# Reordering the seven block products of a second feed-forward product, and building their partner operands in one temporary

## The chip, the cores and the metric

The kernel runs on one core of a Trainium2 chip. The metric is the device time of one execution in microseconds (us); lower is better. TensorE (PE) multiplies, VectorE (DVE), ScalarE (ACT) and GpSimd (POOL) work elementwise, and SyncE (SP) issues most of the transfers.

## The reference

Two encoder layers over 1024 tokens of width 1024, in float32. Layer 0 mixes tokens by windowed attention, layer 1 by a gated linear recurrence (HGRN2); each mixer also has four cross-attention heads into 256 memory tokens. Every layer ends in a feed-forward part with a depthwise convolution of width 3 over tokens. Cut to what matters here:

```python
def conv_ffn(v, w_in, conv_w, conv_b, w_out):          # w_in 1024 x 5632, w_out 2816 x 1024
    gate, up = jnp.split(v @ w_in, 2, axis=-1)
    hid = jax.nn.gelu(dwconv_centred(gate, conv_w, conv_b)) * up
    return hid @ w_out

for layer in range(2):
    u = rmsnorm(h, norm_g[layer, 0])
    y = mixer(u)                                       # layer 0 window attention, layer 1 HGRN2
    h = h + rmsnorm(y, norm_g[layer, 1])
    f = conv_ffn(rmsnorm(h, norm_g[layer, 2]), ...)
    h = h + rmsnorm(f, norm_g[layer, 3])
```

## The kernel before

Every operand of a matmul is split into a rounded high part and the remainder (`wh`/`wl`, `uh`/`ul`: one cast on ACT and one subtraction on DVE), and a float32 product is made of three matmuls, high-high, high-low and low-high.

The program runs start(), window() (layer 0's mixer), its output projection, ffn(0), hgrn() (layer 1's mixer), its output projection and ffn(1). The code gives the instructions in program order; a planner that replays a timeline sets the final order on each engine and lets later work move ahead where its buffers are free. Tiles live in pools that are stacked from the left or the right of SBUF and PSUM, and a pool that is laid on the place of a released one waits tile by tile until the old tiles have been read.

**First feed-forward product** (first_units). The 1024 x 1024 normalised tokens stand transposed in `uh`, `ul`. The first two of 22 column blocks (f = 0, 1) are plain products (plain()). From f = 2 on each block of 128 gate and 128 up columns is computed as seven block products of 12 matmuls (a form of Strassen's method): prod(k, ...) for k = 1, 2, 5, 6, 7, 3, 4. They accumulate in PSUM banks X, V and Y, which ACT or DVE reads between some of them. Their token operands `B[k]` are blocks of `uh`/`ul` or sums of them, made by operands() during f = 0; `B[5]` is written back over a block of `uh`/`ul` at f = 1, once the plain products have read it. Their weight operands are sums too: load(f) brings raw blocks into tiles `sx` and `sy` (two buffers each) by SyncE, and three accumulating DMAs on POOL's queue add to them, one after another; weights() then splits `a1`, `sx`, `sy` and `a22` into ring buffers. conv() and hidden() make the hidden block and store it, with the sums that the second product needs, in DRAM (`hd`).

operands() uses, for each of two halves, three temporaries that take the tags of other tiles: `t3` takes `sy`, `t2` takes `c`, `t4` takes `sx`.

**Second feed-forward product.** The 1024 x 2816 by 2816 x 1024 product is again seven block products M1 to M7, in the order `SECOND`, each over NP2 = 11 units of 256 contraction rows: unit() loads one weight block (or a weight sum made earlier) and one hidden block and splits both; mms() then does 3 matmuls for each of four token tiles t. Four PSUM banks `Xs` stand on the right and four `Vs` on the left. With signs folded into the operands, the quadrants of the result are

```text
c11 = M1 + M2              (early sums:  M1)
c12 = M1 + M6 + M5 + M3    (             M1 + M6)
c22 = M1 + M6 + M7 + M5    (             M1 + M6 + M7)
c21 = M1 + M6 + M7 + M4
```

where c11 and c21 make up the token half `ia`, c12 and c22 the half `ib`. In the order 1 5 6 3 7 2 4, products 1, 6, 7 and 4 accumulate in `Xs`, 5 and 3, and then 2, in `Vs`; between two products on one set of banks lies a product on the other. The half `ib` is complete after product 7, and its four tail() calls (load of the residual rows, scale by the reciprocal root mean square, add, store) run during product 2. The half `ia` ends with product 4: its last LAST units are held back and applied token tile by token tile, so that each tile's tail starts as soon as its own bank is complete. HOLD of the held units have a pool of their own; the others stand in the ring.

In layer 0 (gnext) tail() also normalises the rows for layer 1, and transposes them through a PSUM pool `pst` into `uh`, `ul` (norm_T). `pst` is opened on the left once `Vs` is released after product 2; the transposes of half `ib` are put off to the first units of product 4 (halt, turns). hgrn() then opens its projection banks `psj` (two) on the left and six other banks on the right. Its first work is proj(0): v01 (values and gates of rows 0 to 511), q0, f0 for the first half, then v23, q1 and the rest.

Of the kernel before, what the change touches and what calls it, by code (L numbers as in the profile page):

```python
# [16 lines left out]
P = 128  # L17
# [21 lines left out]
ORD = ["V v01 QF q0 f0 v23 B q1 b1 f1 b0"] + ["QFB q0 f0 q1 b1 f1 b0 v0123"] * 6 + ["QFVB q0 f0 v01 v23 q1 b1|f1|b0"]  # L39


LAST = (7, 10)
HOLD = (5, 8)

PLAIN = 2

# [1 line left out]
def build(tc, A, out):  # L48
# [37 lines left out]
    def split(h, l, src):  # L86
        act.copy(h, src)  # L87
        dve.tensor_tensor(l, src, h.bitcast(F32), op=ALU.subtract)  # L88
# [16 lines left out]
        nc.sync.dma_start(g, src_row.to_broadcast([P, D]))  # L105
        return g

    def norm_T(pl, pst, src, g, dh, dl, t, tag="n", ub=2, halt=False):
        ss = pl.tile([P, 1], F32, tag=tag + "ss", name=tag + "ss")
        u = pl.tile([P, D], F32, tag=tag + "u", bufs=ub, name=tag + "u")  # L110
        sumsq(pl, src, ss, u)
        rs = rstd_of(pl, ss, 1, D, tag)
        dve.scalar_tensor_tensor(u, src, rs[:, 0:1], g, op0=ALU.mult, op1=ALU.mult)
        def turn(pst):
            for b in range(2):
                ps = pst.tile([P, 4, P], F32, tag="pt", name="pt")
                for k in range(4):
                    pe.transpose(ps[:, k, :], u[:, (4 * b + k) * P:(4 * b + k + 1) * P], ident)  # L118
                split(dh[:, 4 * b:4 * b + 4, t * P:(t + 1) * P],
                      dl[:, 4 * b:4 * b + 4, t * P:(t + 1) * P], ps)  # L120

        if halt:
            return turn
        turn(pst)

    w2sum = [dram.tile([NP2, 4, P, 512], F32, name=f"w2s{l}") for l in range(2)]

# [406 lines left out]
    def ffn(l, wo, dst, gnext, halves_, out_halves):  # L534
# [51 lines left out]
        def operands():  # L586

            b12 = (uh[:, :4, tj], ul[:, :4, tj])
            late = []
            for kk in range(2):  # L590
                ks = slice(2 * kk, 2 * kk + 2)
                f32 = lambda x: x[:, ks].bitcast(F32)
                def tmp(t, b=1):
                    return fp.tile([P, 2, 512], F32, tag=t, bufs=b, name=t)
                def both(o, x, y, sub):
                    q = tmp("tt", 2)
                    dve.tensor_tensor(o, f32(x[0]), f32(y[0]), op=ALU.subtract)
                    dve.tensor_tensor(q, f32(x[1]), f32(y[1]), op=ALU.subtract)
                    dve.tensor_tensor(o, o, q, op=ALU.add)
                def more(o, a_, x, op):  # L600
                    dve.tensor_tensor(o, a_, f32(x[0]), op=op)
                    dve.tensor_tensor(o, o, f32(x[1]), op=op)
                t3, t2, t4 = tmp("sy", 2), tmp("c", 3), tmp("sx", 2)
                both(t3, B[3], b12, True)
                split(B[7][0][:, ks], B[7][1][:, ks], t3)
                more(t2, t3, B[1], ALU.add)
                nsplit(B[6][0][:, ks], B[6][1][:, ks], t2)
                more(t4, t2, B[2], ALU.subtract)
                split(B[4][0][:, ks], B[4][1][:, ks], t4)
                e1 = tmp("u") if kk else tmp("g")  # L610
                both(e1, B[1], b12, True)
                late.append((ks, e1))
            return late
# [122 lines left out]
                yield  # L736


        SECOND = (1, 5, 6, 3, 7, 2, 4)
        where = {1: (2, None), 2: (3, None), 4: (1, None), 5: (None, 0), 7: (None, 1), 6: (None, 2), 3: (None, 3)}  # L740
        todo = [(k, p) for k in SECOND for p in range(NP2)]
        made = []
# [1 line left out]
        def unit(k, p):  # L744
            r = stg.tile([P, 2, 512], F32, tag="st", name="st")
            a_, d_ = where[k]
            nc.sync.dma_start(r[:, 0, :], A["ffw2"][l, p, a_] if d_ is None else w2d[p][d_])
            nc.sync.dma_start(r[:, 1, :], hd[k, p])
            pl = hold_pool if k == 4 and 0 <= p - (NP2 - LAST[l]) < HOLD[l] else ring
            h, l_ = [pl.tile([P, 1024], F32R, tag=t, name=t) for t in ("wh", "wl")]  # L750
            r = r.rearrange("p a b -> p (a b)")
            if k == 6:
                nsplit(h[:, :512], l_[:, :512], r[:, :512])
                split(h[:, 512:], l_[:, 512:], r[:, 512:])
            else:
                split(h, l_, r)
            return h, l_

        def second_ahead():
            if todo and len(made) < (LAST[l] if todo[0][0] == 4 else 3):  # L760
                made.append(unit(*todo.pop(0)))

        for _ in first_units():
# [13 lines left out]
        g3 = grow(np_, A["norm_g"][l, 3:4, :], "g3")  # L777
        g0 = grow(np_, A["norm_g"][l + 1, 0:1, :], "g0") if gnext else None
        dve.tensor_scalar_mul(g3[:, 512:], g3[:, 512:], -1.0)
        y = {q: yp.tile([P, 4, 512], F32, name=q) for q in ("c11", "c12", "c22")}  # L780
        ss = {q: yp.tile([P, 4], F32, name=q) for q in ("q11", "q12", "q22")}
        Xs = {t: psl.tile([P, 512], F32, tag=f"x{t}", name="X") for t in (2, 3, 0, 1)}
        Vs = None
        tok = lambda b, t: slice((4 * b + t) * P, (4 * b + t + 1) * P)

        def tail(b, t, ya, sa, yb, sb):


            ts_ = tok(b, t)
            x = np_.tile([P, D], F32, tag="x", bufs=2, name="x")  # L790
            nc.sync.dma_start(x, h1d[l][ts_, :])
            sq = np_.tile([P, 1], F32, tag="sq", name="sq")
            dve.tensor_tensor(sq, sa, sb, op=ALU.add)
            rs = rstd_of(np_, sq, 1, D, "p")
            last = not gnext and b == out_halves[0] and t == 3
            for c, yy in ((slice(0, 512), ya), (slice(512, 1024), yb)):
                dve.scalar_tensor_tensor(x[:, c], yy, rs[:, 0:1], x[:, c], op0=ALU.mult, op1=ALU.add)
                if last:
                    (nc.sync if c.start == 0 else act).dma_start(dst[ts_, c], x[:, c])
            if not last:  # L800
                nc.sync.dma_start(dst[ts_, :], x)
            if gnext:
                return norm_T(np_, pst, x, g0, uh, ul, 4 * b + t, ub=4, halt=True)

        def scaled(q, n, c):

# [8 lines left out]

        ia, ib = out_halves
        D0, D1 = slice(0, 512), slice(512, 1024)
        pst, turns = None, []
        for k in SECOND:
            if k in (5, 2):  # L820
                Vs = [psr.tile([P, 512], F32, tag="v", name="V") for _ in range(4)]
            ps = Xs if k in (1, 6, 7, 4) else Vs
            hold = []
            for p in range(NP2):
                while len(made) < 1:
                    second_ahead()
                h, l_ = made.pop(0)
                second_ahead()
                if k == 4 and p >= NP2 - LAST[l]:
                    hold.append((p, h, l_))  # L830
                else:
                    mms(k, p, h, l_, ps, range(4), k in (1, 5, 2) and p == 0)
                if k == 2 and p in (2, 4, 6, 8):
                    t = p // 2 - 1
                    turns.append(tail(ib, t, y["c12"][:, t, :], ss["q12"][:, t:t + 1],
                                      y["c22"][:, t, :], ss["q22"][:, t:t + 1]))
                if k == 4 and gnext and p < 4:
                    turns.pop(0)(pst)
            for t in range(4):
                if k == 1:  # L840
                    act.copy(y["c11"][:, t, :], Xs[t])
                elif k == 5:
                    act.copy(y["c22"][:, t, :], Vs[t])
                elif k == 6:
                    act.copy(y["c12"][:, t, :], Xs[t])
                elif k in (3, 7, 2):
                    q = {3: "c12", 7: "c22", 2: "c11"}[k]
                    dve.tensor_tensor(y[q][:, t, :], ps[t], y[q][:, t, :], op=ALU.add)
                else:
                    for p, h, l_ in hold:  # L850
                        mms(k, p, h, l_, ps, (t,), False)
                    sb = np_.tile([P, 1], F32, tag="sb", name="sb")
                    y1 = np_.tile([P, 512], F32, tag="y1", name="y1")
                    sumsq(np_, Xs[t], sb)
                    dve.tensor_tensor(y1, Xs[t], g3[:, D1], op=ALU.mult)
                    turn = tail(ia, t, y["c11"][:, t, :], ss["q11"][:, t:t + 1], y1, sb)
                    if gnext:
                        turn(pst)
            if k == 3:
                scaled("c12", "q12", D0)  # L860
            elif k == 7:
                scaled("c22", "q22", D1)
            elif k == 2:
                scaled("c11", "q11", D0)
                psr.release()
                if gnext:
                    pst = tc.alloc_tile_pool(name=f"fnps{l}", bufs=2, space=PSUM, reuse_waits="tile")
        if pst:
            pst.release()
        hold_pool.release()  # L870
# [338 lines left out]
    start()  # L1209
    window()  # L1210
    wo0.finish()
    ffn(0, wo0, h2d, True, (0, 1), (1, 0))
    hgrn()
    wo1.finish()
    ffn(1, wo1, out, False, (1, 0), (1, 0))
# [81 lines left out]
```

## Time and profile before

| | |
|---|---|
| median of 3 runs | 2780.41 us (2777.91 to 2783.5) |
| profiled execution | 2779.65 us, of which the span of instructions is 2777.9 us |
| mean granted TensorE clock | 0.985 |
| busy share of the span: PE, DVE, ACT, POOL | 96%, 66%, 50%, 17% |
| first product of layer 0, layer 1 (with their plain blocks) | about 598 to 1041 us, 2115 to 2560 us |
| second product of layer 0, layer 1 | about 1041 to 1257 us, 2560 to 2770 us |

Times in views of the trace count from the span's start. A row of a timeline gives start and duration in us, engine, line, operation and tiles, and in square brackets how long the engine was idle before and what ended that. L82 to L88 and L118 are helpers that many stages share, so the tile names tell which stage a row belongs to. A matmul of 512 columns is shown with a duration of 0.39 us, but the next one starts 0.227 us after it: matmuls overlap, and the distance of starts is what counts.

### The profile page before, as it was taken

The numbers are of one execution on the slowest core, as the hardware profiler recorded it, in microseconds if no ns is written. First come the engines' busy times: TensorE is split into PE (matmuls) and PEld (weight loads), VectorE is DVE, ScalarE is ACT, GpSimd is POOL, SyncE is SP. The second block draws the span as 40 slices with busy tenths as digits, with TensorE's granted clock in tenths as the row PEclk, the third lists the DMA queues.
The fourth block names the chain that finished last, engine by engine and source line by source line (L and its number), as shares of the span: only waits on it lengthen the run. The fifth ranks groups of instructions, "written<-read, shape, count | busy, mean of one in ns | idle before, by whom it ended". The sixth has DMA issues, their size and how long they took to land.

```text
span 2777.9 us, 39008 instructions
## 1 busy us (share of the span) xinstructions
PE 2678.2 (96%) x14264; PEld 2280.1 (82%) x14264; DVE 1829.5 (66%) x3031; ACT 1389.2 (50%) x2542; POOL 472.6 (17%) x517
## 2 busy tenths in 40 slices
PE   8999999998999999998999999999899899999998
PEld 7888887786888888877898888898788688888887
DVE  6488777676565565575757778778567565656456
ACT  6367667544444445454544455545454344444443
POOL 1231120201111100131212333222120111110013
PEclk9999999999999999998999999999999999999999
DMA  8683212736777857672223642111473777775666
GB/s 281 200 180 77 65 58 86 218 126 163 206 195 197 206 150 245 190 264 84 92 80 130 130 103 62 35 50 43 123 222 115 178 199 204 201 190 175 221 191 234
DMA packets 213584, 428.54 MB, mean 154 GB/s; under 512 B 20368, under 2 KB 77072, under 8 KB 207760
## 3 DMA queue, kind: packets, MB, share of 16 engines
q1 hardware_dynamic: 187264, 333.50, 37.6%
q0 software_dynamic: 23680, 88.09, 15.3%
q10 hardware_dynamic: 2448, 4.46, 0.4%
q8 instruction: 112, 1.84, 0.3%
q14 instruction: 80, 0.66, 0.1%
HBM read 333.17 MB, written 117.96 MB: 162 GB/s over the span
## 4 chain that ended last, share of the span: by engine, by line
PE 84%; DVE 9%; DMA 3%; issue 2%; ACT 2%; POOL 1%; SPq 0%; DVEq 0%; POOLq 0%; ACTq 0%
PE X L531 23%; PE V L531 13%; PE pj L82 7%; PE pj L83 7%; PE pj L84 7%; PE Y L531 4%; PE pb L82 4%; PE pb L83 4%; PE pb L84 3%; PE po L1115 1%; PE pt L343 1%; PE pa L1067 1%; PE pa L1047 1%; PE pu L1091 1%; PE pt L118 1%
## 5 line engine op out<-in xcount | busy, mean ns | idle before, releaser
L88 DVE TENSOR_TENSOR wl<-st,wh 128x1024 fp32r<-128x1024 f32 (+1 forms) x234 | 259.0, 1111 | 330.4 <-ACT wh L87 330.3
L87 ACT CAST wh<-st 128x1024 fp32r<-128x1024 f32 (+1 forms) x234 | 218.6, 937 | 276.5 <-PE X L531 136.8
L82 PE MATMUL pj<-wh,uh 128*128 128x256 f32 (+1 forms) x768 | 235.5, 307 | 0.5 <-DVE ul L88 0.5
L83 PE MATMUL pj<-wl,uh 128*128 128x256 f32 (+1 forms) x768 | 234.9, 306 | 0.0
L84 PE MATMUL pj<-wh,ul 128*128 128x256 f32 (+1 forms) x768 | 234.5, 305 | 0.0
L82 PE MATMUL pj<-uh,wh 128*128 128x512 f32 x512 | 205.6, 402 | 6.6 <-DVE s L969 4.2
L84 PE MATMUL pj<-uh,wl 128*128 128x512 f32 x512 | 203.8, 398 | 0.0
L83 PE MATMUL pj<-ul,wh 128*128 128x512 f32 x512 | 203.7, 398 | 0.0
L531 PE MATMUL V<-uh,wh 128*128 128x512 f32 x344 | 135.7, 394 | 17.9 <-ACT wh L87 17.8
L82 PEld LDWEIGHTS pj<-wh,uh 128*128 128x128 f32 x768 | 148.0, 193 | 2.4 <-DVE ul L88 0.9
L83 PEld LDWEIGHTS pj<-wl,uh 128*128 128x128 f32 x768 | 148.0, 193 | 1.1
L84 PEld LDWEIGHTS pj<-wh,ul 128*128 128x128 f32 x768 | 148.0, 193 | 0.5
L78 DVE TENSOR_TENSOR wl<-st,wh 128x1024 fp32r<-128x1024 f32 (+1 forms) x93 | 116.8, 1262 | 46.9 <-ACT wh L77 46.6
L77 ACT CAST wh<-st 128x1024 fp32r<-128x1024 f32 (+1 forms) x103 | 104.0, 1016 | 70.9 <-PE pj L83 33.7
L531 PE MATMUL X<-wl,wh 128*128 128x512 f32 x352 | 137.3, 391 | 0.2 <-DVE wl L88 0.2
L531 PE MATMUL X<-wh,wl 128*128 128x512 f32 x352 | 137.1, 390 | 0.0
L531 PE MATMUL X<-wh 128*128 128x512 f32 x352 | 136.4, 390 | 0.0
L531 PE MATMUL V<-ul,wh 128*128 128x512 f32 x344 | 135.2, 393 | 0.0
L531 PE MATMUL V<-uh,wl 128*128 128x512 f32 x344 | 134.7, 392 | 0.0
L1061 POOL TENSOR_TENSOR E<-EP,q 128x256 f32<-128x256 f32 x64 | 52.6, 822 | 408.0 <-DVE EP L1054 371.8
L82 PEld LDWEIGHTS pj<-uh,wh 128*128 128x128 f32 x512 | 97.0, 189 | 26.1 <-DVE s L969 4.8
L84 PEld LDWEIGHTS pj<-uh,wl 128*128 128x128 f32 x512 | 97.0, 189 | 19.7
(364 smaller groups left out, 7560.9 us busy)
## 6 DMA issues: line engine op xcount, KB each, us to landing
st<-hid SPq DMA_DIRECT2D x154, 256.0 KB, 3.0
st<-in_ffw_dram SPq DMA_DIRECT2D x106, 256.0 KB, 4.7
w2s<-in_ffw_dram POOLq DMA_DIRECT2D x24, 1024.0 KB, 7.9
st<-in_ffw_dram SPq DMA_DIRECT2D x48, 512.0 KB, 3.8
hid<-tt SPq DMA_DIRECT2D x88, 256.0 KB, 4.6
st<-w2s SPq DMA_DIRECT2D x88, 256.0 KB, 2.7
sy<-in_ffw_dram SPq DMA_DIRECT2D x40, 512.0 KB, 6.1
sx<-in_ffw_dram SPq DMA_DIRECT2D x80, 256.0 KB, 3.8
```

The source lines that it names most:

```text
L77: act.copy(h[:, :n], raw)
L78: (eng or dve).tensor_tensor(l[:, :n], raw, h[:, :n].bitcast(F32), op=ALU.subtract)
L82: pe.matmul(o, ah, bh, start=first, stop=False)
L83: pe.matmul(o, ah, bl, start=False, stop=False)
L84: pe.matmul(o, al, bh, start=False, stop=last)
L87: act.copy(h, src)
L88: dve.tensor_tensor(l, src, h.bitcast(F32), op=ALU.subtract)
L118: pe.transpose(ps[:, k, :], u[:, (4 * b + k) * P:(4 * b + k + 1) * P], ident)
L343: pe.transpose(tp[:, j, :], sm[:, j, c * P:(c + 1) * P], ident)
L531: pe.matmul(o, x, y, start=new, stop=e, skip_group_check=not first)
L1047: pe.matmul(pa[:, c, :], E2[:, cs], E1[:, cs], start=True, stop=True)
L1061: pool.tensor_tensor(gl, pl_, ql, op=ALU.mult)
```

## The change

Four things are edited.

- operands() makes its sums in place, in a single temporary `x` of tag `c` for each half; `sx` and `sy` are no longer borrowed.
- `SECOND` becomes 1 6 7 4 2 5 3. Products 1, 6, 7 and 4 accumulate one after another in `Xs` and are copied out by ACT at each step; 2 goes to `Vs`; 5 and 3 go to `Xs` anew. The half `ia` (c11, c21) is complete after product 2, and its tails run during product 5 (after units 1, 3, 5 and 7), transposes included. The half `ib` ends with product 3, whose last units are held and whose tails add the bank to c12 before they square and scale it.
- `pst` is opened on the right, above `Xs`, and no longer on the left. norm_T loses its deferred form.
- LAST goes from (7, 10) to (6, 10), HOLD from (5, 8) to (4, 7), `y` gets a fourth tile, and in layer 0 out_halves becomes (0, 1), so that rows 0 to 511 are still the ones that end first there.

```diff
-LAST = (7, 10)
-HOLD = (5, 8)
+LAST = (6, 10)
+HOLD = (4, 7)
...
-                t3, t2, t4 = tmp("sy", 2), tmp("c", 3), tmp("sx", 2)
-                both(t3, B[3], b12, True)
-                split(B[7][0][:, ks], B[7][1][:, ks], t3)
-                more(t2, t3, B[1], ALU.add)
-                nsplit(B[6][0][:, ks], B[6][1][:, ks], t2)
-                more(t4, t2, B[2], ALU.subtract)
-                split(B[4][0][:, ks], B[4][1][:, ks], t4)
+                x = tmp("c", 3)
+                both(x, B[3], b12, True)
+                split(B[7][0][:, ks], B[7][1][:, ks], x)
+                more(x, x, B[1], ALU.add)
+                nsplit(B[6][0][:, ks], B[6][1][:, ks], x)
+                more(x, x, B[2], ALU.subtract)
+                split(B[4][0][:, ks], B[4][1][:, ks], x)
...
-        SECOND = (1, 5, 6, 3, 7, 2, 4)
+        SECOND = (1, 6, 7, 4, 2, 5, 3)
...
-        Xs = {t: psl.tile([P, 512], F32, tag=f"x{t}", name="X") for t in (2, 3, 0, 1)}
-        Vs = None
+        left = lambda: {t: psl.tile([P, 512], F32, tag=f"x{t}", name="X") for t in (2, 3, 0, 1)}
+        Xs, Vs = left(), [psr.tile([P, 512], F32, tag="v", name="V") for _ in range(4)]
...
         for k in SECOND:
-            if k in (5, 2):
-                Vs = [psr.tile([P, 512], F32, tag="v", name="V") for _ in range(4)]
-            ps = Xs if k in (1, 6, 7, 4) else Vs
+            if k == 5:
+                Xs = left()
+            ps = Vs if k == 2 else Xs
...
-                if k == 2 and p in (2, 4, 6, 8):
-                    t = p // 2 - 1
-                    turns.append(tail(ib, t, y["c12"][:, t, :], ss["q12"][:, t:t + 1],
-                                      y["c22"][:, t, :], ss["q22"][:, t:t + 1]))
-                if k == 4 and gnext and p < 4:
-                    turns.pop(0)(pst)
+                if k == 5 and p in (1, 3, 5, 7):
+                    t = p // 2
+                    tail(ia, t, y["c11"][:, t, :], ss["q11"][:, t:t + 1], y["c21"][:, t, :], ss["q21"][:, t:t + 1])
             for t in range(4):
...
+                if k in (1, 6, 7, 4):
+                    act.copy(y[{1: "c11", 6: "c12", 7: "c22", 4: "c21"}[k]][:, t, :], ps[t])
+                elif k in (2, 5):
+                    q = y[{2: "c11", 5: "c22"}[k]][:, t, :]
+                    dve.tensor_tensor(q, ps[t], q, op=ALU.add)
                 else:
                     for p, h, l_ in hold:
                         mms(k, p, h, l_, ps, (t,), False)
...
-                    sumsq(np_, Xs[t], sb)
-                    dve.tensor_tensor(y1, Xs[t], g3[:, D1], op=ALU.mult)
-                    turn = tail(ia, t, y["c11"][:, t, :], ss["q11"][:, t:t + 1], y1, sb)
-                    if gnext:
-                        turn(pst)
+                    dve.tensor_tensor(y1, ps[t], y["c12"][:, t, :], op=ALU.add)
+                    sumsq(np_, y1, sb)
+                    dve.tensor_tensor(y1, y1, g3[:, D0], op=ALU.mult)
+                    tail(ib, t, y1, sb, y["c22"][:, t, :], ss["q22"][:, t:t + 1])
...
                 psr.release()
                 if gnext:
-                    pst = tc.alloc_tile_pool(name=f"fnps{l}", bufs=2, space=PSUM, reuse_waits="tile")
+                    pst = tc.alloc_tile_pool(name=f"fnps{l}", bufs=2, space=PSUM, side="right", reuse_waits="tile")
...
-    ffn(0, wo0, h2d, True, (0, 1), (1, 0))
+    ffn(0, wo0, h2d, True, (0, 1), (0, 1))
```

More of the change, by code (lines that the diff above doesn't have):

```diff
@@ L106, in grow, with norm_T @@
         return g
-    def norm_T(pl, pst, src, g, dh, dl, t, tag="n", ub=2, halt=False):
+    def norm_T(pl, pst, src, g, dh, dl, t, tag="n"):
         ss = pl.tile([P, 1], F32, tag=tag + "ss", name=tag + "ss")
-        u = pl.tile([P, D], F32, tag=tag + "u", bufs=ub, name=tag + "u")
+        u = pl.tile([P, D], F32, tag=tag + "u", name=tag + "u")
         sumsq(pl, src, ss, u)
@@ L113, in norm_T @@
         dve.scalar_tensor_tensor(u, src, rs[:, 0:1], g, op0=ALU.mult, op1=ALU.mult)
[L114 to L123, printed above, removed]
-        turn(pst)
+        for b in range(2):
+            ps = pst.tile([P, 4, P], F32, tag="pt", name="pt")
+            for k in range(4):
+                pe.transpose(ps[:, k, :], u[:, (4 * b + k) * P:(4 * b + k + 1) * P], ident)
+            split(dh[:, 4 * b:4 * b + 4, t * P:(t + 1) * P],
+                  dl[:, 4 * b:4 * b + 4, t * P:(t + 1) * P], ps)
     w2sum = [dram.tile([NP2, 4, P, 512], F32, name=f"w2s{l}") for l in range(2)]
@@ L748, in unit @@
             nc.sync.dma_start(r[:, 1, :], hd[k, p])
-            pl = hold_pool if k == 4 and 0 <= p - (NP2 - LAST[l]) < HOLD[l] else ring
+            pl = hold_pool if k == 3 and 0 <= p - (NP2 - LAST[l]) < HOLD[l] else ring
             h, l_ = [pl.tile([P, 1024], F32R, tag=t, name=t) for t in ("wh", "wl")]
@@ L759, in second_ahead @@
         def second_ahead():
-            if todo and len(made) < (LAST[l] if todo[0][0] == 4 else 3):
+            if todo and len(made) < (LAST[l] if todo[0][0] == 3 else 3):
                 made.append(unit(*todo.pop(0)))
@@ L779, in ffn @@
         dve.tensor_scalar_mul(g3[:, 512:], g3[:, 512:], -1.0)
-        y = {q: yp.tile([P, 4, 512], F32, name=q) for q in ("c11", "c12", "c22")}
-        ss = {q: yp.tile([P, 4], F32, name=q) for q in ("q11", "q12", "q22")}
-        Xs = {t: psl.tile([P, 512], F32, tag=f"x{t}", name="X") for t in (2, 3, 0, 1)}
-        Vs = None
+        y = {q: yp.tile([P, 4, 512], F32, name=q) for q in ("c11", "c21", "c12", "c22")}
+        ss = {q: yp.tile([P, 4], F32, name=q) for q in ("q11", "q21", "q22")}
+        left = lambda: {t: psl.tile([P, 512], F32, tag=f"x{t}", name="X") for t in (2, 3, 0, 1)}
+        Xs, Vs = left(), [psr.tile([P, 512], F32, tag="v", name="V") for _ in range(4)]
         tok = lambda b, t: slice((4 * b + t) * P, (4 * b + t + 1) * P)
@@ L794, in tail @@
             rs = rstd_of(np_, sq, 1, D, "p")
-            last = not gnext and b == out_halves[0] and t == 3
+            last = not gnext and b == out_halves[1] and t == 3
             for c, yy in ((slice(0, 512), ya), (slice(512, 1024), yb)):
@@ L802, in tail @@
             if gnext:
-                return norm_T(np_, pst, x, g0, uh, ul, 4 * b + t, ub=4, halt=True)
+                norm_T(np_, pst, x, g0, uh, ul, 4 * b + t)
         def scaled(q, n, c):
@@ L817, in ffn @@
         D0, D1 = slice(0, 512), slice(512, 1024)
-        pst, turns = None, []
+        pst = None
         for k in SECOND:
-            if k in (5, 2):
-                Vs = [psr.tile([P, 512], F32, tag="v", name="V") for _ in range(4)]
-            ps = Xs if k in (1, 6, 7, 4) else Vs
+            if k == 5:
+                Xs = left()
+            ps = Vs if k == 2 else Xs
             hold = []
@@ L828, in ffn @@
                 second_ahead()
-                if k == 4 and p >= NP2 - LAST[l]:
+                if k == 3 and p >= NP2 - LAST[l]:
                     hold.append((p, h, l_))
@@ L832, in ffn @@
                     mms(k, p, h, l_, ps, range(4), k in (1, 5, 2) and p == 0)
-                if k == 2 and p in (2, 4, 6, 8):
-                    t = p // 2 - 1
-                    turns.append(tail(ib, t, y["c12"][:, t, :], ss["q12"][:, t:t + 1],
-                                      y["c22"][:, t, :], ss["q22"][:, t:t + 1]))
-                if k == 4 and gnext and p < 4:
-                    turns.pop(0)(pst)
-            for t in range(4):
[L840 to L848, printed above, removed]
+                if k == 5 and p in (1, 3, 5, 7):
+                    t = p // 2
+                    tail(ia, t, y["c11"][:, t, :], ss["q11"][:, t:t + 1], y["c21"][:, t, :], ss["q21"][:, t:t + 1])
+            for t in range(4):
+                if k in (1, 6, 7, 4):
[3 more added lines that the diff above has]
+                    dve.tensor_tensor(q, ps[t], q, op=ALU.add)
                 else:
@@ L853, in ffn @@
                     y1 = np_.tile([P, 512], F32, tag="y1", name="y1")
-                    sumsq(np_, Xs[t], sb)
-                    dve.tensor_tensor(y1, Xs[t], g3[:, D1], op=ALU.mult)
-                    turn = tail(ia, t, y["c11"][:, t, :], ss["q11"][:, t:t + 1], y1, sb)
-                    if gnext:
[L858 to L861, printed above, removed]
+                    dve.tensor_tensor(y1, ps[t], y["c12"][:, t, :], op=ALU.add)
+                    sumsq(np_, y1, sb)
+                    dve.tensor_tensor(y1, y1, g3[:, D0], op=ALU.mult)
+                    tail(ib, t, y1, sb, y["c22"][:, t, :], ss["q22"][:, t:t + 1])
+            if k == 4:
+                scaled("c21", "q21", D1)
+            elif k == 5:
                 scaled("c22", "q22", D1)
```

## The prediction, made before the change was run

> **What bounds the kernel now.** I read the page's busy times and its chain first, then TensorE's idle places, then the two stages that the diff touches. Parts 1 and 4 of the page:
>
> ```profile
> PE 2678.2 (96%) x14264; PEld 2280.1 (82%) x14264; DVE 1829.5 (66%) x3031; ACT 1389.2 (50%) x2542; POOL 472.6 (17%) x517
> PE 84%; DVE 9%; DMA 3%; issue 2%; ACT 2%; POOL 1%; SPq 0%; DVEq 0%; POOLq 0%; ACTq 0%
> ```
>
> TensorE carries the time. The change takes no matmul away, so it can only win or lose where TensorE stands still or runs at a lower clock. The windows view, three stretches (PE busy with its number of matmuls first; PEclk is the number after POOL's pair), and one row of the chain in order of time:
>
> ```profile
> 1060.00:1160.00 100.00, 100.00 (x443) 82.84 (x442) 47.32 (x51) 46.05 (x61) 0.00 (x0) 1.00 0.67 218
> 640.00:700.00 60.00, 49.50 (x198) 38.76 (x197) 32.86 (x34) 24.64 (x32) 11.33 (x13) 0.89 0.81 195
> 2155.00:2215.00 60.00, 46.38 (x188) 36.97 (x187) 33.88 (x34) 23.22 (x29) 10.48 (x12) 0.89 0.73 181
> 1071.17 29.92 PE V L531 x132
> ```
>
> A block product of 132 matmuls takes 29.92 us, 0.227 each. At that rate the 198 matmuls of 640 to 700 need 44.9 us: 15.1 are lost. In the second layer 188 need 42.7: 17.3 are lost. Both stretches are where the two plain column blocks of the first feed-forward product end and the seven-product form begins (f = 2). The second product itself (1060 to 1160) loses nothing. TensorE's timeline at the first of them, and the queues behind it (start, duration, instruction, idle time before and its releaser):
>
> ```profile
> 645.63 0.39 PE L531 MATMUL X<-uh,wl 128*128 128x512 f32 x1
> 653.31 0.80 PE L531 MATMUL V<-uh,wh 128*128 128x512 f32 x1 [7.29 <-ACT wh L87]
> 664.79 0.52 PE L531 MATMUL X<-u6h,wh 128*128 128x512 f32 x1 [3.11 <-ACT wh L87]
> 639.69 1.22 DVE L88 TENSOR_TENSOR u4l<-sx,u4h 128x1024 fp32r<-128x1024 f32 x1
> 640.95 4.21 SPq L623 DMA_DIRECT2D sx<-in_ffw_dram  x4
> 645.83 0.94 POOL L626 DMA_DIRECT2D sx<-in_ffw_dram  x1 [41.27 <-DMA sx<-in_ffw_dram]
> 652.22 1.04 ACT L87 CAST wh<-sx 128x1024 fp32r<-128x1024 f32 x1 [4.58 <-DMA sx<-in_ffw_dram]
> 663.70 1.04 ACT L87 CAST wh<-sy 128x1024 fp32r<-128x1024 f32 x1 [4.55 <-DMA sy<-sy]
> 2162.57 0.39 PE L531 MATMUL X<-uh,wl 128*128 128x512 f32 x1
> 2173.50 0.79 PE L531 MATMUL V<-uh,wh 128*128 128x512 f32 x1 [10.54 <-ACT wh L87]
> ```
>
> The weight sums of f = 2 are built in tiles sx and sy. operands() borrows the same tags, so SyncE can load sx only when VectorE has read its last operand out of it (639.69 + 1.22, load at 640.95). From there load, three accumulating DMAs and casts take until 663.70, 22.8 us, and TensorE waits for the sx cast and then the sy cast.
>
> The third place is between the layers (timelines of TensorE and VectorE, with two rows of the chain, which give the step from one matmul to the next):
>
> ```profile
> 1256.79 0.39 PE L531 MATMUL X<-wh,wl 128*128 128x512 f32 x1
> 1257.02 0.60 PE L118 MATMUL pt<-ident,nu 128*128 128x128 f32 x4
> 1265.73 1.97 PE L118 MATMUL pt<-ident,nu 128*128 128x128 f32 x8 [5.72 <-DVE ul L88]
> 1274.33 0.69 DVE L88 TENSOR_TENSOR ul<-pt,uh 128x512 fp32r<-128x512 f32 x1 [1.23 <-ACT uh L87]
> 1275.08 0.58 PE L82 MATMUL pj<-wh,uh 128*128 128x256 f32 x1 [0.55 <-DVE ul L88]
> 1275.88 0.21 PE pj L84
> 1279.81 0.12 PE pj L82
> 1242.77 1.23 DVE L78 TENSOR_TENSOR wl<-st,wh 128x1024 fp32r<-128x1024 f32 x1 [0.71 <-ACT wh L77]
> ```
>
> From the last matmul of the second product to the first projection of layer 1 there are 18.3 us with nothing but transposes. That projection (v01) reads rows 0 to 511, which are long ready, and its weights are split by 1244.0. It starts 0.06 us after VectorE has emptied a transpose bank: psj lies on the PSUM banks of pst. The 32 transposes in between are work, 0.11 each (four in 0.60, of which the last one's own time is some 0.28): 3.5. So 14.8 are lost, and about twenty projection matmuls start 0.21 apart instead of 0.12, 1.9 more: 16.7.
>
> **The change, part by part.**
>
> Operands in one temporary. It uses tag c alone; sx and sy are free when the pool opens. The same DVE and ACT instructions remain. Moved are, for f = 2 and 3, three SyncE loads and three POOL accumulations each:
>
> ```profile
> 603.37 0.78 SPq L541 DMA_DIRECT2D cb<-in_conv_b_dram  x1
> 622.78 5.95 SPq L624 DMA_DIRECT2D sy<-in_ffw_dram  x2
> 604.01 0.55 POOL L94 TENSOR_TENSOR nrs<-nms,nhalf 128x1 f32<-128x1 f32 x1 [2.96 <-DVE nms L92]
> 645.97 1.23 DVE L599 TENSOR_TENSOR u<-u,tt 128x1024 f32<-128x1024 f32 x1
> 612.00:648.00 36.00, 34.02 (x150) 27.69 (x148) 35.16 (x33) 13.86 (x16) 0.94 (x1) 1.00 0.23 71
> 2168.14 1.22 DVE L88 TENSOR_TENSOR ul<-u,uh 128x1024 fp32r<-128x1024 f32 x1
> ```
>
> SyncE has nothing between 604.2 and 622.8, POOL nothing between 604.6 and 645.8, so the loads can go out near 605 and the 22.8 us chain ends near 628, 18 us ahead of 645.9, where TensorE has used up what it holds. Were POOL to take an accumulation before its last power (604.01), that norm would slip by one load at most, 3.8 us; I take 0, since the plain blocks start on other rows. What is late next is VectorE: it is busy 35.16 of 36 us from 612 to 648, its last operand for product 5 ends at 647.2, then one cast (1.04) and one subtraction (1.22) follow: 649.5. The weight splits of f = 2, formerly behind that, may now stand ahead of it: 1.22 + 1.22 + 0.69 = 3.1 more, 652.6. Writing in place makes VectorE wait for each cast before it overwrites: three hand-overs of 1.05 per half, 6.3 for the two halves if nothing covers them; I take 0, because the two halves and the first convolution interleave. TensorE meanwhile has products 6 and 7, 24 matmuls, 5.4 us. With two bank hand-overs at 1.55 (below) these end at 654.4, when product 5's operand is there: what remains in layer 0 is the 3.1 of the hand-overs. In layer 1 that operand is complete at 2169.4 even now, with the splits 2172.5, and TensorE has used up what it holds at 2162.8: 2172.5 - 2162.8 - 5.4 = 4.3. Ends: 0 and 10 each. Gain: 15.1 - 3.1 = 12.0 and 17.3 - 4.3 = 13.0.
>
> The order 1 6 7 4 2 5 3 with pst on the right. The two projection banks (left) now follow the V banks, which VectorE empties after product 2, two products before the end. TensorE can run v01 (96 matmuls at 0.12: 11.5 us) and q0, f0 (24 each at 0.227: 10.9) while the last rows are normalised; 22.4 us stand against the 18.3 that the tail took. So the 16.7 go but for about 2.5, because q and f weights need ring buffers that the held units free only at the end (a cast and a subtraction, 1.04 + 1.22, ahead of them): 14.2. Ends: 0 (the planner leaves the projections behind) and 16.7.
>
> What the order costs. Four switches per layer (1 to 6, 6 to 7, 7 to 4, 5 to 3) now accumulate on into banks that ACT or VectorE must first read; before, a product on the other banks lay between. The trace has one such hand-over with nothing between:
>
> ```profile
> 1036.46 0.39 PE L531 MATMUL X<-u7h,wl 128*128 128x512 f32 x1
> 1038.24 0.50 PE L531 MATMUL X<-u4h,wh 128*128 128x512 f32 x1 [1.39 <-ACT g L722]
> 665.17 0.58 ACT L716 COPY s<-V 128x512 f32<-128x512 f32 x1
> 1188.85 0.69 DVE L848 TENSOR_TENSOR c<-X,c 128x512 f32<-128x512 f32 x1 [1.09 <-PE X L531]
> 1195.00:1225.00 30.00, 30.00 (x134) 24.86 (x133) 25.04 (x33) 14.71 (x21) 12.52 (x11) 1.00 0.86 296
> ```
>
> It costs 1.78 - 0.23 = 1.55. In the new order each bank is covered by the three others, 9 matmuls, 2.04 us, so the first three switches are free unless a cast of 1.04 stands ahead of the copy (1.55 + 1.04 - 2.04, about 0.5). ACT gets four more copies of 0.58 per layer; it is busy 46 of 100 us there, so nothing. The switch 5 to 3 needs VectorE while it carries the tails, 25 of 30 us in the like stretch before: 0 to 3. I take 1 per layer, 2 together, ends 0 and 9. Six held units instead of seven shorten each last step by 3 matmuls, and move work, no time.
>
> The end. ACT's square sum waited for TensorE alone; now VectorE adds first, and it is still in the tail of the tile before:
>
> ```profile
> 2769.88 0.40 PE L531 MATMUL X<-wh,wl 128*128 128x512 f32 x1
> 2770.36 0.60 ACT L101 ACTIVATE junk<-X 128x512 bf16<-128x512 f32 x1 [5.90 <-issue]
> 2770.38 0.75 DVE L797 SCALAR_TENSOR_TENSOR x<-y,prs,x 128x512 f32<-128x512 f32 x1
> 2771.69 0.15 DVE L793 TENSOR_TENSOR sq<-q,sb 128x1 f32<-128x1 f32 x1
> ```
>
> The add runs 2771.1 to 2771.75, the square sum and its read 0.8 more, so the step of 2771.69 comes at 2772.6: +0.9 (0.6 to 2); the product with g3 goes beside POOL's power.
>
> Sum: 2779.65 (the profiled execution; span 2777.9, 0.8 under the median 2780.41) - 12.0 - 13.0 - 14.2 + 2 + 0.9 = 2743.4. I take 2743.
>
> A rule against the first part: the Trainium skill, SBUF — State Buffer, section "Who interferes with whom", says that a DMA issued by GpSimd can find no port for its descriptors while VectorE holds the shared pair. The moved accumulations would run beside a VectorE that is 98% busy. The row that bears on it, all accumulations of this line (min/median/max in ns):
>
> ```profile
> L626 POOL DMA_DIRECT2D sx<-in_ffw_dram x40: 864/868/1162, 645.8 to 2504.6; - x40
> ```
>
> At most 0.3 us of delay each, six of them under 2 us, within the 18 us by which the chain is early. By the page at its worst they would wait for VectorE's end near 647, and the gain of this part would be lost; that is the second rival.
>
> **The rivals.** First, the planner keeps v01 behind the last transposes, or its ACT and DVE work holds them up: 14.2 lost, 2757. For it: ACT and DVE are both in the tail then. Against: in this trace the projection starts the moment its bank is free.
> Second, the weight chain is not early: sx and sy wait on something else (space of the pools before, or POOL's descriptors). 25.0 lost, 2768. Against: 41.27 us in which POOL waits for this load and nothing else.
> Third, slower: the hand-overs are not covered, since copies queue behind casts and adds behind tails. 4 switches, 4 banks, 2 layers at 1.55 is 49.6 instead of 2: 2791. It decides from an average of (38.3 + 5.6) / 32, about 1.4 us per hand-over.
>
> **How the numbers follow.** The runs span 5.6 us, 0.2%: less is no change. My case has 0.70 (2733 to 2753); first rival 0.12; second 0.10; third 0.04; 0.04 for both of the first two together, about 2782, no change. Faster: 0.92; same 0.04; slower 0.04. The lower bound is all three losses gone, 2780 - 49 = 2731. The range 2730 to 2762 takes in the first rival and leaves out 0.18.
>
> **What would show it.** The sx load near 605 instead of 640.95; VectorE or its B5 halves, not a weight cast, named at TensorE's first gap behind the plain blocks, of under 5 us; projections among the last transposes, with no gap over 2 us; gaps under 0.6 us at the first three switches; the last square sum released by VectorE. The prediction is wrong if the planner orders the tails so that VectorE becomes the bound in product 5, or if layer 1's recurrence, which starts earlier against its loads, gives the lead back.

## The result, and the profile after

| | median | runs | ratio to before, 95% interval |
|---|---|---|---|
| before, same chip | 2779.23 us | 2777.91 to 2783.5 | |
| changed kernel | 2736.74 us | 2734.76 to 2739.04 | 0.9845 (0.9828 to 0.9862) |

The change takes 42.5 us, 1.5%. Predicted were 2743 us, 36.2 less than the median before. The profiled execution has a span of 2733.8 us, so the two profiles are 44.1 apart. Parts 1 and 4 of the page after:

```profile
PE 2663.9 (97%) x14264; PEld 2269.8 (83%) x14264; DVE 1830.0 (67%) x3031; ACT 1392.6 (51%) x2550; POOL 471.0 (17%) x517
PE 88%; DVE 7%; DMA 2%; issue 1%; ACT 1%; POOL 1%; SPq 0%; DVEq 0%; POOLq 0%; ACTq 0%
```

The number of matmuls is the same, 14264, and so is VectorE's work. ACT has the eight copies more. In the chain TensorE's share rises from 84 to 88%; VectorE gives up two points of that, and DMA, ACT and issue one or so each.

To see where the time went, I cut the span at the same instructions in both profiles (us):

| stretch | before | after | difference |
|---|---|---|---|
| start to the first feed-forward product | 598.25 | 594.77 | -3.5 |
| plain blocks and first product, layer 0 | 442.61 | 428.26 | -14.4 |
| second product, layer 0, to its last matmul | 215.92 | 217.08 | +1.2 |
| from there through layer 1's mixer to its feed-forward part | 858.75 | 843.60 | -15.2 |
| plain blocks and first product, layer 1 | 444.55 | 429.36 | -15.2 |
| second product, layer 1, to its last matmul | 209.79 | 211.30 | +1.5 |
| last matmul to the end | 8.00 | 9.39 | +1.4 |

The first row isn't the change: up to there every engine has the same instructions in the same order. Over the ten profiles of this study this stretch takes 593.9 to 598.3 us; one and the same kernel, profiled twice, took 597.9 and 594.4, so the spread is not the kernel's. The other rows are the change, and they add up to -40.6.

The stretches that answer to those of before, in the windows view (PE busy with its matmuls first, then PEld, DVE, ACT, POOL, the granted clock, the DMA share and GB/s):

```profile
640.00:700.00 60.00, 59.55 (x262) 48.50 (x261) 45.27 (x48) 31.22 (x41) 6.93 (x8) 1.00 0.64 169
2120.00:2180.00 60.00, 58.33 (x255) 47.34 (x254) 48.93 (x50) 31.20 (x40) 6.34 (x8) 1.00 0.60 158
1030.00:1172.00 142.00, 142.00 (x628) 117.57 (x628) 69.48 (x70) 68.41 (x90) 6.52 (x4) 1.00 0.66 218
```

At 0.227 us each the 262 matmuls need 59.5 us and the 255 need 57.9: about 0.5 and 2.1 us are lost, where 15.1 and 17.3 were. The clock is 1.00 where it was 0.89. The third stretch holds products 1, 6, 7 and 4, and so the first three switches of layer 0: 142 us, 142 busy.

What the queues did in the first of these places (timelines of SyncE, POOL, ACT, VectorE and TensorE, as before):

```profile
602.42 0.80 SPq L618 DMA_DIRECT2D sx<-in_ffw_dram  x2
607.72 0.94 POOL L621 DMA_DIRECT2D sx<-in_ffw_dram  x1 [6.65 <-ACT uh L87]
611.78 0.87 POOL L621 DMA_DIRECT2D sx<-in_ffw_dram  x1 [3.12 <-issue]
615.62 0.87 POOL L622 DMA_DIRECT2D sy<-sx  x1 [2.97 <-DMA sx<-in_ffw_dram]
623.06 1.05 ACT L87 CAST wh<-sx 128x1024 fp32r<-128x1024 f32 x1 [2.19 <-PE Y L526]
634.17 1.05 ACT L87 CAST wh<-sy 128x1024 fp32r<-128x1024 f32 x1 [6.07 <-PE V L526]
618.06 0.60 ACT L577 ACTIVATE g<-V 128x512 f32<-128x512 f32 x1 [9.24 <-PE V L526]
619.97 1.28 DVE L556 SCALAR_TENSOR_TENSOR c<-g,ncw,c 128x1023 f32<-128x1023 f32 x1 [5.50 <-ACT c L555]
624.64 1.22 DVE L88 TENSOR_TENSOR wl<-sx,wh 128x1024 fp32r<-128x1024 f32 x1
640.00 1.22 DVE L88 TENSOR_TENSOR ul<-g,uh 128x1024 fp32r<-128x1024 f32 x1
645.15 1.22 DVE L88 TENSOR_TENSOR ul<-u,uh 128x1024 fp32r<-128x1024 f32 x1
653.50 1.22 DVE L88 TENSOR_TENSOR u4l<-c,u4h 128x1024 fp32r<-128x1024 f32 x1
642.36 0.39 PE L526 MATMUL V<-uh,wh 128*128 128x512 f32 x1
643.20 0.50 PE L526 MATMUL X<-u6h,wh 128*128 128x512 f32 x1 [0.45 <-ACT s L688]
```

The sx load goes out at 602.42 and no longer at 640.95, and its cast stands at 623.06 where it was 652.22. TensorE runs on from the plain blocks into products 5 (V) and 6 (X) with one short wait, for ACT's copy of a bank.

Between the layers (timeline of TensorE):

```profile
1240.11 0.39 PE L526 MATMUL X<-wh,wl 128*128 128x512 f32 x1
1240.34 0.28 PE L82 MATMUL pj<-wh,uh 128*128 128x256 f32 x1
1240.45 0.28 PE L83 MATMUL pj<-wl,uh 128*128 128x256 f32 x1
1241.17 0.60 PE L117 MATMUL pt<-ident,nu 128*128 128x128 f32 x4
```

The first projection starts 0.23 us after the last matmul of the second product, where it was 18.3 us. The transposes stand between projections, and those follow each other at 0.11.

### The profile page after: what moved, and what is told of

Read it like the earlier page. It is cut to its first block, busy times and chain, and to the rows that moved or that the text cites. A ratio compares the mean times of both kernels' runs of the same rounds, so it can differ in the third digit from the quotient of the medians.

```text
span 2733.8 us, 39013 instructions
## 1 busy us (share of the span) xinstructions
PE 2663.9 (97%) x14264; PEld 2269.8 (83%) x14264; DVE 1830.0 (67%) x3031; ACT 1392.6 (51%) x2550; POOL 471.0 (17%) x517
## 4 chain that ended last, share of the span: by engine, by line
PE 88%; DVE 7%; DMA 2%; issue 1%; ACT 1%; POOL 1%; SPq 0%; DVEq 0%; POOLq 0%; ACTq 0%
PE X L526 27%; PE V L526 11%; PE pj L82 8%; PE pj L84 7%; PE pj L83 7%; PE Y L526 5%; PE pb L83 4%; PE pb L82 4%; PE pb L84 4%; PE po L1101 1%; PE pa L1053 1%; PE pt L338 1%; PE pa L1033 1%; PE pt L117 1%; PE pu L1077 1%
## 5 line engine op out<-in xcount | busy, mean ns | idle before, releaser
L526 PE MATMUL X<-wl,wh 128*128 128x512 f32 x528 | 205.1, 390 | 1.4 <-DVE wl L88 1.4
L526 PE MATMUL X<-wh,wl 128*128 128x512 f32 x528 | 205.0, 390 | 0.0
L526 PE MATMUL X<-wh 128*128 128x512 f32 x528 | 200.4, 390 | 2.1 <-DVE c L835 2.1
L526 PEld LDWEIGHTS X<-wh 128*128 128x128 f32 x528 | 99.1, 188 | 23.9 <-issue 2.9
```

Source lines behind the costliest of these rows:

```text
L526: pe.matmul(o, x, y, start=new, stop=e, skip_group_check=not first)
```

## The experiments

The theory is the prediction's account: separate causes, two of them gains (sx and sy free early; the projection banks no longer on those of the transposes), and a small cost of the new order. What could stand in its place, beside what single expectations name: the gain of the operands comes from writing in place, not from which tags are borrowed; the gain between the layers comes from the order (the early end of one half), and the place of `pst` alone gives little; the new order is itself worth something. "The new order" stands below for the order together with what came with it (LAST, HOLD, the fourth tile of `y`, out_halves); these were not run apart.

**Operands alone.** The kernel before with the one hunk in operands():

```diff
-                t3, t2, t4 = tmp("sy", 2), tmp("c", 3), tmp("sx", 2)
+                x = tmp("c", 3)
...
```

> The kernel before with the in-place operands alone. Theory (the operand edit works by leaving tiles sx and sy free, the bank edit by leaving the projection banks free, and the two add up): the losses behind the plain blocks go in both layers, 14.4 and 15.2 us as in the changed kernel, the 18 us between second product and first projection stay: about 2750. Rival (the edits only pay together, because the time won in the first product is waited for again at the end of the second): under 10 us gained, 2770 or more.

Measured: 2748.49 us (2746.21 to 2752.77), ratio 0.9888 (0.9873 to 0.9902). The two feed-forward stretches are 428.2 and 429.3 us, those of the changed kernel to 0.1; 18.33 us stay between last matmul and first projection. The windows view and TensorE's timeline between the layers:

```profile
640.00:700.00 60.00, 59.55 (x262) 48.55 (x261) 45.32 (x48) 31.23 (x41) 7.80 (x9) 1.00 0.65 171
1238.54 0.39 PE L531 MATMUL X<-wh,wl 128*128 128x512 f32 x1
1256.87 0.58 PE L82 MATMUL pj<-wh,uh 128*128 128x256 f32 x1 [0.55 <-DVE ul L88]
```

The row of the window is that of the changed kernel, and the wait between the layers that of before. The part stands by itself.

**Order and transposes alone.** The changed kernel with the old operands:

```diff
-                x = tmp("c", 3)
+                t3, t2, t4 = tmp("sy", 2), tmp("c", 3), tmp("sx", 2)
...
```

> The changed kernel with the old operands (three temporaries in the tags sy, c, sx). Theory: the losses of 15 and 17 us behind the plain blocks are back, the lead at the start of layer 1 stays (15 us), less some 3 us that the new order costs at the switch 5 to 3 and at the end: about 2767. Rival: no lead without the operand edit, about 2780.

Measured: 2770.29 us (2767.31 to 2771.86), ratio 0.9964 (0.9951 to 0.9977), 3 us above what was expected. Both feed-forward stretches are back at 442.1 and 446.2, and the projection starts 0.23 us after the last matmul. The windows view, and timelines of SyncE and TensorE:

```profile
640.00:700.00 60.00, 49.40 (x200) 38.92 (x199) 31.28 (x33) 24.08 (x32) 11.33 (x13) 0.91 0.82 200
638.67 4.21 SPq L618 DMA_DIRECT2D sx<-in_ffw_dram  x4
2157.32 0.79 PE L526 MATMUL V<-uh,wh 128*128 128x512 f32 x1 [10.77 <-ACT wh L87]
```

Load at 638.67, clock 0.91 and a wait of 10.77 us for a weight cast: the picture of before.

**The transposes' banks alone.** The kernel before with one argument more, in the old order:

```diff
-pst = tc.alloc_tile_pool(name=f"fnps{l}", bufs=2, space=PSUM, reuse_waits="tile")
+pst = tc.alloc_tile_pool(name=f"fnps{l}", bufs=2, space=PSUM, side="right", reuse_waits="tile")
```

> The kernel before, old order 1 5 6 3 7 2 4 and old operands, with the transpose pool pst on the right alone: one argument. Theory (the bank alone held the projection back): the first projection starts within 1 us of the second product's last matmul instead of 18.3 us later, 15 us gained: about 2764, and the order of the products isn't needed for it. Rival (the order is what counts: rows 0 to 511 must be finished, transposes included, a product earlier): the projection still starts only among or after the last transposes, under 3 us gained: 2776 to 2780.

Measured: 2762.73 us (2760.79 to 2764.5), ratio 0.9937 (0.9922 to 0.9952). TensorE's timeline:

```profile
1255.41 0.39 PE L531 MATMUL X<-wh,wl 128*128 128x512 f32 x1
1255.63 0.28 PE L82 MATMUL pj<-wh,uh 128*128 128x256 f32 x1
1256.35 0.38 PE L118 MATMUL pt<-ident,nu 128*128 128x128 f32 x2
```

The wait of 18.3 us is gone in the old order too. The place of the banks is enough, and that the gain there needs the order falls.

**The order without the place.** The changed kernel with `pst` back on the left (the reverse of that line):

> The changed kernel with pst back on the left, all else as changed. Theory (the projection waits for the PSUM banks that it shares with the transposes): the 18 us without projections between the second product and layer 1 are back, 15 us lost against the changed kernel: about 2752. Rival (finishing the first half two products early, transposes included, is enough): 2737.

Measured: 2754.66 us (2753.72 to 2756.08), ratio 0.9915 (0.9902 to 0.9929). Timelines of VectorE and TensorE:

```profile
1260.22 0.69 DVE L88 TENSOR_TENSOR ul<-pt,uh 128x512 fp32r<-128x512 f32 x1 [1.29 <-ACT uh L87]
1260.96 0.58 PE L82 MATMUL pj<-wh,uh 128*128 128x256 f32 x1 [0.55 <-DVE ul L88]
```

The projection waits for a transpose bank again, 19.90 us behind the last matmul. So the new order without the new place brings nothing there, and this kernel is no better than the one with the operands alone (ratio 0.9888; the intervals touch at 0.9902). Against that kernel's profile, the stretch between the layers is 3.0 us longer and the end 1.9; another 2.95 lie in the common start, which varies.

**Both gains, old order.** The kernel before with the operands and `pst` on the right, nothing else:

> The kernel before with the in-place operands and pst on the right, old order of the products. Theory: all of the gain without the new order, and without its stall at the switch 5 to 3 (2.3 and 1 us in the changed kernel) and its longer end (1.4): 2733 to 2737, the changed kernel's time or up to 3 us less. Rival (the order counts): 2750.

Measured: 2733.49 us (2730.25 to 2735.09), ratio 0.983 (0.9814 to 0.9847): no slower than the whole change, so the new order brings no gain of its own. The same kernel and the changed one were then run once more, side by side on one chip:

> The changed kernel again, beside the next one on the same chip: 2737, to compare with.

> In-place operands and pst on the right with the old order of the products, again, in five rounds beside the changed kernel. Theory (the new order costs the stall at the switch 5 to 3 and a longer end in each layer, and brings nothing): 3 to 5 us less than the changed kernel, about 2733. Rival (the difference seen in separate sets of runs was the scatter between chips): within 1 us of the changed kernel.

Measured: changed kernel 2734.5 us (2731.58 to 2740.48), ratio 0.9845 (0.983 to 0.986); old order 2731.24 us (2729.36 to 2732.08), ratio 0.9831 (0.9818 to 0.9845). The intervals of the ratios overlap, so the times alone don't settle the 3 us. Two terms can be compared over all profiles: the second product of layer 1 takes 211.1 to 212.8 us in three of the four profiles with the new order and 210.4 in the fourth, against 209.7 to 210.6 in the six with the old; the end takes 9.4 to 9.6 us against 7.7 to 8.3. For the end the loss is shown; for the second product the ranges overlap. The old order with both other parts is the version to keep, as far as these runs tell.

**In place, but in a borrowed tile.** The kernel before with the one temporary in `sx`, so that sy is free and sx is not:

```diff
-                t3, t2, t4 = tmp("sy", 2), tmp("c", 3), tmp("sx", 2)
+                x = tmp("sx", 2)
...
```

> The kernel before with operands in place in one temporary, as in the change, but in tag sx, so that the borrowed tile is still one that the weight loads need. Theory (only the tag matters): the sx load of f = 2 still goes out near 641 and TensorE still loses 15 and 17 us behind the plain blocks: 2776 to 2785. Rival (fewer temporaries or the order that VectorE gets from working in place is what helps): 2750, as with tag c.

Measured: 2778.36 us (2776.73 to 2780.02), ratio 0.9999 (0.999 to 1.0008). Timelines of SyncE and TensorE, and the windows view:

```profile
602.19 0.80 SPq L624 DMA_DIRECT2D sy<-in_ffw_dram  x2
637.12 0.80 SPq L623 DMA_DIRECT2D sx<-in_ffw_dram  x2
658.72 0.79 PE L531 MATMUL X<-u6h,wh 128*128 128x512 f32 x1 [6.59 <-ACT wh L87]
2169.22 0.80 PE L531 MATMUL V<-uh,wh 128*128 128x512 f32 x1 [9.17 <-ACT wh L87]
640.00:700.00 60.00, 50.93 (x203) 40.37 (x202) 29.90 (x31) 23.29 (x32) 11.31 (x13) 0.89 0.81 202
```

The sy loads go out at 602.19, the sx loads only at 637.12, and TensorE waits as before. Writing in place is worth nothing as long as sx is borrowed: that sx comes free decides. It is the head of the chain (sx adds into the first half of sy, and that into the second), so sy alone being free doesn't help. Whether sx alone would be enough, with sy borrowed, wasn't tried.

## Why the prediction was right, point by point

**Operands: the mechanism was right, the size too small by 4.5 us.** 12.0 and 13.0 were predicted, 14.4 and 15.2 came, and the part alone gave the same 14.4 and 15.2. The loads left at 602.42 (predicted near 605), and the first accumulation was in before the sx cast of 623.06. The sy cast, the last step of the chain, was predicted near 628 and ran at 634.17, where its row names TensorE and not the chain as what held it; both casts are well ahead of 645.9. The terms mis-sized are the remainders, 3.1 and 4.3, where the window counts leave about 0.5 and 2.1. In them:
- I let product 5 wait for its whole operand, with both weight splits ahead of it: 652.6. The splits did move ahead (624.64, and 636.00 for sy), but the operand was ready at 646.4 (645.15 + 1.22). VectorE put off the last operands of product 4 instead: u4l ended at 644.3 before, and now runs 653.50 to 654.7. No wait of TensorE goes back to it.
- Product 5 needs the first half of its operand only to start, and TensorE did start at 642.36, behind the `ul<-g` of 640.00. From there products 5 and 6 alternate, so the bank hand-over costs 0.84 - 0.23 = 0.6 where I took twice 1.55.
- The in-place hand-overs were taken as 0, and by themselves they are. The kernel that writes in place in `sx` keeps VectorE busy for 31.97 of the 32 us from 608 to 640 (row below). In the changed kernel VectorE did stand 5.50 us before 619.97, in the row for the convolution's activation `c` (L555): there ACT ran the first cast of the operand (619.85) only behind its copy of bank V, for which it had waited 9.24 us, while with `sx` that cast came ahead of the copy, at 614.18. Why the planner ordered ACT so is open. VectorE's lead was large enough to hide it.

In place in `sx`, windows view (VectorE is the third pair):

```profile
608.00:640.00 32.00, 32.00 (x143) 26.32 (x142) 31.97 (x31) 12.56 (x14) 0.00 (x0) 1.00 0.07 24
```

In layer 1 three short waits are left, for a copy, a cast and the operand of product 6 (TensorE's timeline):

```profile
2131.81 0.50 PE L526 MATMUL X<-u6h,wh 128*128 128x512 f32 x1 [0.45 <-ACT s L688]
2133.73 0.49 PE L526 MATMUL V<-uh,wh 128*128 128x512 f32 x1 [0.27 <-ACT uh L87]
2135.17 0.50 PE L526 MATMUL X<-u6l,wh 128*128 128x512 f32 x1 [0.95 <-DVE u6l L550]
```

**The rule on VectorE and GpSimd's descriptors, weighed in the prediction, did not decide.** The accumulation of 607.72, the first of f = 2, and that of 611.78, the first of f = 3, fall beside VectorE's two-input float32 operations, back to back from 608.71 to 614.48. They took 0.94 and 0.87 us to issue, no more than before. The next link of the f = 2 chain, 615.62, waits for the landing of the first and follows it by 7.90 us; in the kernel before, the same two links lie 6.66 us apart (645.83 in the prediction's rows, and the row below), with VectorE standing still from 647.2 to 653.29. That is 1.2 us more at most, with other loads in flight at the time, against a lead of 18.

```profile
652.49 0.86 POOL L627 DMA_DIRECT2D sy<-sx  x1 [5.71 <-DMA sx<-in_ffw_dram]
```

The prediction took the rule in the section "Who interferes with whom" of the Trainium skill, SBUF — State Buffer, wider than it is: the section says that its probe saw DMAs stall beside `tensor_copy` and not beside `tensor_tensor`, which is what ran here. The trace agrees, and the second rival falls.

**The projection banks: right, 15.2 against 14.2.** This is the stretch's whole difference, costs of the new order within it; with the old order it was 17.8 in the kernel with the banks alone, and 16.5 and 17.0 in the two profiles with both parts, about the whole 16.7 and not the 14.2 of it that I allowed. What was not seen is that the order plays no part: I argued that the projection banks follow the V banks, emptied two products before the end, but in the old order, with the banks on the right, the wait goes too. The first rival falls.

**The switches: +1.2 and +1.5 against 1 each, and the nearness is in part luck.** The first three cost nothing in either layer: 142 of 142 us busy in layer 0 as shown, and as many from 2520 to 2662 in layer 1. The switch 5 to 3 costs in layer 0 what VectorE's queue makes it (timelines of TensorE and VectorE; the last row is of layer 1):

```profile
1205.70 0.39 PE L526 MATMUL X<-wh,wl 128*128 128x512 f32 x1
1208.18 0.47 PE L526 MATMUL X<-wh 128*128 128x512 f32 x1 [2.09 <-DVE c L835]
1205.01 1.28 DVE L113 SCALAR_TENSOR_TENSOR nu<-x,nrs,g 128x1024 f32<-128x1024 f32 x1 [0.73 <-POOL nrs L94]
1206.21 1.22 DVE L88 TENSOR_TENSOR wl<-st,wh 128x1024 fp32r<-128x1024 f32 x1
1207.35 0.68 DVE L835 TENSOR_TENSOR c<-X,c 128x512 f32<-128x512 f32 x1
2696.31 0.50 PE L526 MATMUL X<-wl,wh 128*128 128x512 f32 x1 [0.77 <-DVE wl L88]
```

The add that frees the bank stands behind a row of the other half's normalisation and a weight split, so TensorE loses 2.48 - 0.23 = 2.25. In the four profiles with the new order this wait costs 1.7 to 2.3 us. Yet the whole stretch is 215.6 to 215.9 us in the other three of them, and 215.8 to 216.4 in the six with the old order, which waits at other places of its last product: in layer 0 the new order costs nothing that repeats, and the +1.2 is this one profile's. In layer 1 the switch itself costs 0.1 us here and between 0 and 2.3 us over the four; most of the +1.5 is the wait of 2696.31 for a weight split, ten matmuls later, which the prediction did not have. The third rival, 1.4 us at all 32 hand-overs, falls.

**The end: +1.4 against +0.9** (timelines of VectorE and ACT):

```profile
2725.74 0.68 DVE L841 TENSOR_TENSOR y<-X,c 128x512 f32<-128x512 f32 x1
2726.51 0.63 ACT L101 ACTIVATE junk<-y 128x512 bf16<-128x512 f32 x1 [5.45 <-DVE y L841]
2727.27 0.69 DVE L843 TENSOR_TENSOR y<-y,g 128x512 f32<-128x512 f32 x1 [0.85 <-ACT junk L101]
2727.88 0.15 DVE L787 TENSOR_TENSOR sq<-sb,q 128x1 f32<-128x1 f32 x1
```

The add and ACT's square sum came as predicted. The step that failed is the product with g3: it overwrites `y`, so it waits for the square sum, and then it stands ahead of the sq add on VectorE. I had put it beside POOL's power. That is the 0.6 between 2727.27 and 2727.88.

**The sum.** The terms were 39.2 of gain and 2.9 of cost, and came out as 44.7 and 4.1. Of the 6.3 us between 2743 and the median (the errors of the two gains all went the same way), 4.5 are the two remainders and 1.0 the transition, less 1.2 more of cost; the 2 that are left are within the spread of the common start.

## What to carry to other kernels

A tile that is borrowed for a while delays the next load into it: look for the first transfer of a pipeline that leaves late, see which reader of the tile releases it, and give the borrower a tile that nothing early needs; here 30 of the 42 us hung on borrowed tags, and freeing sy without sx brought nothing. A PSUM pool stacked on another waits for that one's last reader, so the place of a small pool of transposes can cost a later stage 18 us, and a better place is worth more than a new order of products. When a change has several parts, run each alone: here two small edits carry the gain, and the largest one brings nothing and adds 1.4 us at the end.

## What the runs showed of the hardware

A wait can cost TensorE more than its length. In the kernel before, the matmul of 653.31 in the prediction's rows comes after 7.29 us of standing still. The next two start 0.60 and 0.66 us apart, most of those behind them 0.43, and the usual 0.23 is back from 658.3 on; the granted clock of that stretch is 0.50. After the 2.09 us wait of 1208.18 shown above, the changed kernel's next one starts after 0.30, and the one behind that at the usual 0.23. The windows view of before, and TensorE's timelines, two rows of before and three of after:

```profile
648.10:658.20 10.10, 4.85 (x10) 3.09 (x11) 4.76 (x4) 4.31 (x6) 2.61 (x3) 0.50 0.74 122
653.91 0.63 PE L531 MATMUL V<-ul,wh 128*128 128x512 f32 x1
654.57 0.79 PE L531 MATMUL V<-uh,wl 128*128 128x512 f32 x1
1208.48 0.39 PE L526 MATMUL X<-wl,wh 128*128 128x512 f32 x1
1208.71 0.40 PE L526 MATMUL X<-wh,wl 128*128 128x512 f32 x1
326.68 0.53 PE L82 MATMUL pj<-uh,wh 128*128 128x512 f32 x1 [2.49 <-DVE xl L88]
```

This fits Part 1, "The HAM clock gate", of the Trainium skill, TensorE: Matmul & The Clock Gate, by which a window of some 3.4 us without work takes the clock to half. The traces differ from it in one point: a shorter wait can be enough. In the changed kernel the 2.49 us before 326.68 are followed by steps of 0.43 us as well, but the 2.96 us before 1519.59 by the usual 0.23, so the length of a single wait does not decide it here. The prediction's losses hold this cost, since they were counted from matmuls done and not from the gaps.

Second, the same instructions in the same order took 593.9 to 598.3 us up to the first feed-forward product, a spread as large as the smaller terms of this change. So these had to be read stage by stage, and over several profiles.
